# One-hot weights with tokens innermost, and expert and last-layer sums kept by tokens

## The chip, the cores and the metric

The program runs on one core of a Trainium2 chip. The metric is device time in microseconds (us). Three runs of the kernel before took 1616.15, 1618.21 and 1618.53 us; the median is 1618.21 us. The names of the engines are those of the profile: PE is TensorE (PEld its weight loads), DVE VectorE, ACT ScalarE, POOL GpSimd, SP the queue that issues the DMAs.

## The reference

Two transformer blocks run on 256 tokens with 1024 features, in float32.

The first block has a gated convolution and a chunkwise mLSTM, then the layer `peer`: 8 heads each pick 16 of 16384 experts per token. With `u` and `v` the two expert tables it computes

```
z   = einsum('thkd,td->thk', take(u, e), h)
a   = gelu(z) * g                      # g: softmax weights of the picked experts
out = einsum('thk,thkd->td', a, take(v, e))
x   = x + g2 * rms_norm(out, norm2_post)
```

The second block is stick-breaking attention beside a gated linear recurrence, then an MLP, `x = x + square(relu(rms_norm(x) @ w_up)) @ w_down`, whose result is the output.

## The kernel before

**Layout and arithmetic.** An activation is held with features on the 128 partitions and the 256 tokens along the free dimension, as 8 slices of 128x256. A float32 product is made of three matmuls in the format fp32r: a weight piece of 128x1024 is read by DMA (`raw`), ACT rounds it to a high half `wh` (line 164), and DVE, or POOL for the pieces named in `pool_`, subtracts to get the low half `wl` (line 165). `mm3` (lines 184 to 186) then adds wh·xh, wh·xl and wl·xh. Three `wh`/`wl` buffers rotate.

**The peer layer.** The kernel doesn't gather experts; it goes densely through all 16384 in 128 chunks of 128. `z_chunk` (line 847) makes the 128x256 scores of a chunk with 24 matmuls (`gemm`) and ACT applies gelu. `out_chunks` (line 1063) splits a scaled chunk into `ah`, `al` and adds its part of the output with `acc_k` (line 238): for each of 8 feature slices three matmuls, the weights being 128x128 pieces of `wh` or `wl`, the moving operand the 256 tokens of `ah` or `al`. The sums stand in four PSUM banks, two feature slices of 128x256 in each.

Between the two the scores are multiplied by the routing weights of each token and expert. `weights_of(s, n)` (line 1016) builds them for n groups of 32 chunks, in 16 blocks of TB=16 tokens: DVE makes a one-hot `o1` of the first key with the keys innermost (line 1023), a one-hot `o2` of the second key with the tokens innermost (line 1027) and `og`, two products of `o2` with the high and the low part of the weight (line 1031). For each token one fp16 matmul (line 1038) has `o1` of this token as weights and both parts of `og` as moving operand, 64 columns with n=1 and 128 with n=2; neighbouring columns of `og` are 16 elements (32 bytes) apart. ACT reads one part from PSUM (line 1041), DVE adds the other (line 1042) and multiplies into the scores (line 1046).

`weights_of` is a generator: each `advance(bg, n)` after a chunk runs it on by n steps (n may be a fraction, which is saved up), and `drain(bg)` runs what is left. It has 3 steps a block with n=1 and 4 with n=2. The order is: z chunks 44 to 95 with weights_of(0,1) and 1 step a chunk (NW), drain; out chunks 0 to 31 and z chunks 96 to 127 with weights_of(1,2) and 0.8 steps a chunk (NX), drain; out chunks 32 to 95 with weights_of(3,1) and 1 step (NY), drain; out chunks 96 to 127. These are the stretches from about 558 to 740, 740 to 994, 994 to 1163 and 1163 to 1298 us of the profile.

**The end of the peer layer.** Squares of the eight slices are summed (`presum`, `sums`), the norm is made on one row per token and spread to 128 partitions by matmuls (`norm`, with `fill` matmuls around it, F2), and `residual` adds the slices to x; `scaled` makes the halves of the next gemm's input (lines 321 and 322). The first six weight pieces of that gemm have their low halves made on POOL (LB), and their casts are ordered behind steps of the norm.

**The last layer.** The MLP makes 32 chunks of hidden features, `acc_k` adds them to the output (line 1353), and `finish` (line 1364) multiplies the sums of two slices by the norm `r4`, adds x and issues the output DMA, in the order in which the last two chunks' matmuls end. The output is written with features on partitions and turned on the host.

The instructions of each engine run in its program order; `issue_after` puts one behind another where the code says so.

Of the kernel before, what the change touches and what calls it, by code (L numbers as in the profile page):

```python
# [111 lines left out]
def body(ctx: ExitStack, tc: tile.TileContext, a: dict):  # L112
# [705 lines left out]
    with ExitStack() as p2:  # L818
# [197 lines left out]
        def weights_of(s, n):  # L1016


            m = 32 * n
            for b in range(S // TB):  # L1020
                ts_ = slice(b * TB, (b + 1) * TB)
                o1 = op_.tile([128, TB, 128], F16, tag="o1", name="o1", bufs=2)
                V.tensor_tensor(out=o1, in0=row16[:, None, :].to_broadcast([128, TB, 128]),  # L1023
                                in1=idxT[:, 0, ts_, None].to_broadcast([128, TB, 128]), op=ALU.is_equal)
                yield
# [3 lines left out]
                og = op_.tile([128, 2, 64, TB], F16, tag="og", name="og", bufs=2)[:, :, :m]  # L1029
                for i in range(2):  # L1030
                    V.tensor_tensor(out=og[:, i], in0=o2, in1=gT[:, i, None, ts_].to_broadcast([128, m, TB]),
                                    op=ALU.mult)
                yield
                nt = 8 // n
                for k in range(TB // nt):
                    ps = gt().rearrange("p (t i n) -> p t i n", i=2, n=m)
                    for t in range(nt):
                        T.matmul(ps[:, t], lhsT=o1[:, k * nt + t, :], rhs=og[:, :, :, k * nt + t], start=True, stop=True)  # L1038
                    t0 = b * TB + k * nt
                    u = m2.tile([128, 256], F32, tag="u", name="u", bufs=2).rearrange("p (n t) -> p n t", t=nt)  # L1040
                    A.activation(u, ps[:, :, 0].rearrange("p t n -> p n t"), AF.Copy, scale=1.0 / GS)
                    V.scalar_tensor_tensor(out=u, in0=ps[:, :, 1].rearrange("p t n -> p n t"), scalar=1.0 / GS, in1=u,  # L1042
                                           op0=ALU.mult, op1=ALU.add)
                    for q_ in range(n):
                        zz = zt[s + q_][:, :, t0:t0 + nt]
                        V.tensor_mul(zz, zz, u[:, 32 * q_:32 * q_ + 32])
                    if k % 2:
                        yield
# [56 lines left out]
        total = presum(m2, acc, 6)
        last, mm = sums(m2, ssy, acc, total, 6)
        add = added[0]
        ry, _, root, inv, end = norm(m2, ssy, gt(), mm, F2)
        places = dict(q=(A, last), r=(A, root), e=(A, end), a=(V, add), i=(V, inv), n=(A, None))
        hh3, hl3 = halves()  # L1110
        residual(m2, x, acc, ry, prm[:, 24:32], lambda j: scaled(x, KS("n12"), hh3, hl3, j))

    with ExitStack() as p3:
# [223 lines left out]
        for n in range(32):  # L1339
# [11 lines left out]
            if 0 < n < 30 or n == 31:  # L1351
                k = min(n - 1, 29)
                acc_k(acc, (next(cd), mid[k]), first=k == 0)
            if n == 4:
                total = presum(m3, x)
            if n == 8:
                ssx = pz.tile([128, 384], F32, tag="zr", name="ssx", bufs=1)[:, :256]
                squares(m3, ssx, x, total)
                r4 = m3.tile([128, 256], F32, name="r4")
                V.tensor_scalar(out=r4, in0=ssx, scalar1=1.0 / D, scalar2=EPS, op0=ALU.mult, op1=ALU.add)  # L1360
# [1 line left out]
        adds = []

        def finish(j):

            if j in (0, 2, 4):
                return
            at = slice(j if j > 5 else j - 1, j + 1)
            n = at.stop - at.start
            y = (zs8, e8)[j // 2 % 2].rearrange("p h c t -> p (h c t)")[:, :n * 256].rearrange("p (j t) -> p j t", j=n)  # L1370
            with tc.issue_after(adds[-1].ins) if adds else ExitStack():
                V.tensor_tensor(out=y, in0=acc.t[j // 2][:, at.start % 2:at.start % 2 + n], op=ALU.mult,
                                in1=r4[:, None, :].to_broadcast([128, n, 256]))
            adds.append(V.tensor_add(x[:, at], x[:, at], y))
            SY.dma_start(out=a["out"].rearrange("p (j t) -> p j t", j=8)[:, at], in_=x[:, at])

        acc_k(acc, *[(next(cd), mid[k]) for k in (30, 31)], last=True, order=(6, 0, 1, 2, 3, 4, 5, 7), then=finish)


# [105 lines left out]
```

## Time and profile before

| what | us |
|---|---|
| runs: lowest, median, highest | 1616.15, 1618.21, 1618.53 |
| the profiled execution's own time | 1615.83 |
| its span | 1614.0 |
| PE busy | 1536.8 |
| DVE busy | 1235.1 |
| ACT busy | 762.0 |
| POOL busy | 243.6 |

The mean granted TensorE clock of the profiled execution is 0.972 of full speed. The span goes from the first to the last instruction that the profile records; 1.8 us of the execution lie outside. Busy times are sums over an engine's instructions where they overlap only once. Matmuls are pipelined, so one is recorded with some 280 ns although the next starts after some 118 ns: the rate is read from the starts of neighbours, not from the durations.

### The profile page before, as it was taken

How to read it: one execution, taken by the hardware profiler on the slowest of the kernel's cores; microseconds unless marked ns; L12 is line 12 of the kernel's file. 1: busy time of each engine (PE TensorE's matmuls, PEld its weight loads, DVE VectorE, ACT ScalarE, POOL GpSimd, SP SyncE). 2: the span in 40 equal slices, each digit the busy share in tenths (PEclk: the TensorE clock that was granted, in tenths of full speed). 3: DMA queues.
4: the chain of work that ended last, by engine and by line, in shares of the span. 5: the costliest groups of instructions: out<-in, count | busy, mean ns of one | idle time of the engine just before them, and what ended most of it. 6: DMA issues, size and time to landing. Idle time of an engine off the chain costs nothing.

```text
span 1614.0 us, 29532 instructions
## 1 busy us (share of the span) xinstructions
PE 1536.8 (95%) x12164; PEld 1475.0 (91%) x12164; DVE 1235.1 (77%) x2231; ACT 762.0 (47%) x1263; POOL 243.6 (15%) x109
## 2 busy tenths in 40 slices
PE   5899999989888999999999997999999989999998
PEld 4898899979888999999899985999999979899998
DVE  8978796677969999887877778888755578666555
ACT  3544454445435434444444443444444458754442
POOL 3300000034436843330000000000000030000000
PEclk7999999999999999999999997999999989999999
DMA  9456594534433534444434341444455535344542
GB/s 347 178 196 240 204 336 175 185 120 169 168 132 134 182 134 153 150 144 161 173 134 154 134 156 51 157 153 145 159 191 190 183 121 183 105 155 186 183 184 79
DMA packets 40025, 269.82 MB, mean 167 GB/s; under 512 B 4433, under 2 KB 5201, under 8 KB 9170
## 3 DMA queue, kind: packets, MB, share of 16 engines
q1 hardware_dynamic: 38882, 264.67, 45.5%
q10 hardware_dynamic: 1008, 3.27, 0.6%
q8 instruction: 95, 1.56, 0.4%
q14 instruction: 40, 0.33, 0.1%
HBM read 266.87 MB, written 1.05 MB: 166 GB/s over the span
## 4 chain that ended last, share of the span: by engine, by line
PE 83%; DVE 14%; ACT 2%; issue 1%; DMA 0%; SPq 0%; DVEq 0%; ACTq 0%
PE mm L184 12%; PE mm L186 12%; PE mm L185 12%; PE acc L185 10%; PE acc L186 10%; PE acc L184 10%; PE g L1038 7%; DVE wl L165 1%; DVE cand L877 1%; DVE scr L411 1%; DVE x L342 1%; DVE pr L917 1%; DVE o L1023 1%; PE mm L218 1%; DVE i L871 1%
## 5 line engine op out<-in xcount | busy, mean ns | idle before, releaser
L164 ACT CAST wh<-raw 128x1024 fp32r<-128x1024 f32 x449 | 470.0, 1049 | 623.6 <-PE mm L185 315.1
L165 DVE TENSOR_TENSOR wl<-raw,wh 128x1024 fp32r<-128x1024 f32 x361 | 441.8, 1229 | 175.8 <-ACT wh L164 173.1
L186 PE MATMUL mm<-hh,wl 128*128 128x256 f32 x1816 | 516.4, 284 | 12.3 <-DVE wl L165 12.0
L184 PE MATMUL mm<-hh,wh 128*128 128x256 f32 x1816 | 521.5, 287 | 4.4 <-ACT z L854 4.4
L185 PE MATMUL mm<-hl,wh 128*128 128x256 f32 x1816 | 513.4, 283 | 0.0
L186 PEld LDWEIGHTS mm<-hh,wl 128*128 128x128 f32 x1816 | 346.6, 191 | 15.0 <-DVE wl L165 13.7
L184 PEld LDWEIGHTS mm<-hh,wh 128*128 128x128 f32 x1816 | 345.9, 190 | 11.3 <-ACT z L854 4.6
L185 PEld LDWEIGHTS mm<-hl,wh 128*128 128x128 f32 x1816 | 346.6, 191 | 0.8 <-issue 0.2
L165 POOL TENSOR_TENSOR wl<-raw,wh 128x1024 fp32r<-128x1024 f32 x89 | 227.1, 2558 | 492.5 <-PE mm L312 252.8
L184 PE MATMUL acc<-ah,wh 128*128 128x256 f32 x1024 | 289.4, 283 | 2.0 <-ACT ah L248 2.0
L185 PE MATMUL acc<-al,wh 128*128 128x256 f32 x1024 | 288.6, 282 | 0.0
L186 PE MATMUL acc<-ah,wl 128*128 128x256 f32 x1024 | 288.4, 282 | 0.0
L184 PEld LDWEIGHTS acc<-ah,wh 128*128 128x128 f32 x1024 | 194.6, 190 | 3.9 <-ACT ah L248 2.5
L185 PEld LDWEIGHTS acc<-al,wh 128*128 128x128 f32 x1024 | 193.9, 189 | 0.3
L186 PEld LDWEIGHTS acc<-ah,wl 128*128 128x128 f32 x1024 | 193.3, 189 | 0.0
L1023 DVE TENSOR_TENSOR o<-row,idxT 128x2048 f16<-128x2048 f16 x48 | 123.7, 2577 | 66.1 <-PE g L1038 66.1
L1038 PE MATMUL g<-og,o 128*128 128x64 f16 (+1 forms) x768 | 129.9, 334 | 12.2 <-DVE u L1042 6.5
L1038 PEld LDWEIGHTS <-o 128*128 128x128 f16 x768 | 83.0, 115 | 38.9 <-issue 8.1
L1138 POOL MEMSET q<- 128x2048 f32 x1 | 1.8, 1809 | 557.7 <-DVE al L249 557.7
L185 PE MATMUL acc<-ml,wh 128*128 128x256 f32 x256 | 72.3, 283 | 0.0
L186 PE MATMUL acc<-mh,wl 128*128 128x256 f32 x256 | 72.2, 282 | 0.0
L184 PE MATMUL acc<-mh,wh 128*128 128x256 f32 x256 | 71.9, 282 | 0.0
(435 smaller groups left out, 2194.9 us busy)
## 6 DMA issues: line engine op xcount, KB each, us to landing
raw<-in_uT_dram SPq DMA_DIRECT2D x64, 1024.0 KB, 4.8
raw<-in_ev_dram SPq DMA_DIRECT2D x64, 1024.0 KB, 4.8
araw<-in_wada_dram SPq DMA_DIRECT2D x16, 1024.0 KB, 5.8
raw<-in_wup_dram SPq DMA_DIRECT2D x16, 1024.0 KB, 4.7
raw<-in_wdn_dram SPq DMA_DIRECT2D x16, 1024.0 KB, 4.8
raw<-in_wcxb_dram SPq DMA_DIRECT2D x12, 1024.0 KB, 4.8
araw<-in_wada_dram SPq DMA_DIRECT2D x16, 512.0 KB, 9.9
raw<-in_wout_dram SPq DMA_DIRECT2D x8, 1024.0 KB, 4.8
```

The costliest lines, as they stand in the source:

```text
L164: by.copy(wh, raw) if by is A else by.tensor_copy(wh, raw)
L165: on.tensor_sub(wl, raw, wh)
L184: T.matmul(ps, lhsT=wh, rhs=xh, start=start, stop=False, skip_group_check=skip)
L185: T.matmul(ps[:, :n], lhsT=wh, rhs=xl, start=False, stop=False, skip_group_check=skip)
L186: return T.matmul(ps, lhsT=wl, rhs=xh, start=False, stop=stop, skip_group_check=skip)
L218: T.matmul(ps, lhsT=w, rhs=xh[:, k, :n], start=k == 0, stop=False)
L342: V.tensor_add(x[:, j, :], x[:, j, :], u)
L411: return V.scalar_tensor_tensor(out=scr, in0=raw, scalar=0.5, in1=crow, op0=ALU.mult, op1=ALU.mult, accum_out=ada[:, j:j + 1])
L871: V.max_index(out=ti[:, i, 8:16], in_max=tv[:, i, 8:16], in_values=rep)
L877: V.tensor_add(cand[:, :, o:o + n], tv2[:, :, 0, ra:ra + 1].to_broadcast([128, 2, n]), tv2[:, :, 1, 0:n])
L1023: V.tensor_tensor(out=o1, in0=row16[:, None, :].to_broadcast([128, TB, 128]), in1=idxT[:, 0, ts_, None].to_broadcast([128, TB, 128]), op=A ...
L1038: T.matmul(ps[:, t], lhsT=o1[:, k * nt + t, :], rhs=og[:, :, :, k * nt + t], start=True, stop=True)
```

## The change

The one-hot of the first key is made by DVE with the tokens innermost (`os`) and turned by an ACT copy into `o1`; the weighted one-hots are made by one DVE instruction for both parts (`ow`) and turned by ACT into `og`, whose columns then lie side by side. The block is 8 tokens. Per token there are two matmuls, one for each part, which add up in PSUM, so that one DVE instruction scales the sum and multiplies it into the scores; ACT's read of PSUM is gone. A block is made one block ahead of its matmuls, and a generator has 64 steps. POOL no longer makes low halves after piece 49 of `uT`.

The sums of the experts and of the last layer are kept by tokens: `acc_tok` has a 128x128 piece of `xh` or `xl` (128 tokens) as weights and 512 columns of `wh` or `wl` as moving operand, 12 matmuls a chunk. The end of the peer layer takes the norm per token half with ACT's accumulated squares, scales, turns the result back with 16 transposes, and adds it to x in halves of 128 tokens. The last layer turns x instead (`turn`, 16 transposes and 8 ACT copies during chunks 12 to 19), and writes its output by tokens.

```diff
-TB = 16
+TB = 8
-LB = ('qaee',(0,1,2,3,4,5))
+LB = ('', ())
-F2 = (5,10)
+F2 = 10
-NZ, NR, NW, ZR, NX, NY = (7, 1.75, 1, 44, 0.8, 1)
+NZ, NR, NW, ZR, NX, NY = (7, 1.75, 1.25, 44, 1.05, 1.05)
+    def acc_tok(acc, *steps, first=False, last=False, then=lambda t, c: None):
+        for t in range(2):
+            ts_ = slice(t * 128, (t + 1) * 128)
+            for c in range(2):
+                cs = slice(c * 512, (c + 1) * 512)
+                for n, ((wh, wl), (xh, xl)) in enumerate(steps):
+                    T.matmul(acc[t][c], lhsT=xh[:, ts_], rhs=wh[:, cs], start=first and n == 0, stop=False)
+                    T.matmul(acc[t][c], lhsT=xl[:, ts_], rhs=wh[:, cs], start=False, stop=False)
+                    T.matmul(acc[t][c], lhsT=xh[:, ts_], rhs=wl[:, cs], start=False, stop=last and n == len(steps) - 1)
+                then(t, c)
...
         def weights_of(s, n):
             m = 32 * n
-            for b in range(S // TB):
-                o1 = op_.tile([128, TB, 128], F16, tag="o1", name="o1", bufs=2)
-                V.tensor_tensor(out=o1, in0=row16[:, None, :].to_broadcast([128, TB, 128]),
-                                in1=idxT[:, 0, ts_, None].to_broadcast([128, TB, 128]), op=ALU.is_equal)
...
+            def made_of(b):
+                os = op_.tile([128, 128, TB], F16, tag="os", name="os", bufs=1)
+                V.tensor_tensor(out=os, in0=io16, in1=idxT[:, 0, None, ts_].to_broadcast([128, 128, TB]),
+                                op=ALU.is_equal)
+                o1 = op_.tile([128, TB, 128], F16, tag="o1", name="o1", bufs=2)
+                A.copy(o1, os.rearrange("p n t -> p t n"))
                 o2 = ...
+                ow = op_.tile([128, 2, 64, TB], F16, tag="ow", name="ow", bufs=1)[:, :, :m]
+                V.tensor_tensor(out=ow, in0=o2[:, None].to_broadcast([128, 2, m, TB]),
+                                in1=gT[:, :, None, ts_].to_broadcast([128, 2, m, TB]), op=ALU.mult)
+                og = op_.tile([128, TB, 128], F16, tag="og", name="og", bufs=2)[:, :, :2 * m]
+                og = og.rearrange("p t (i n) -> p t i n", i=2)
+                A.copy(og, ow.rearrange("p i n t -> p t i n"))
+                return o1, og
+            blocks = S // TB
+            next_ = made_of(0)
+            yield
+            for b in range(blocks):
+                o1, og = next_
+                if b + 1 < blocks:
+                    next_ = made_of(b + 1)
+                    yield
+                ps = gt()[:, :TB * m].rearrange("p (t n) -> p t n", t=TB)
+                for t in range(TB):
+                    for i in range(2):
+                        T.matmul(ps[:, t], lhsT=o1[:, t, :], rhs=og[:, t, i], start=i == 0, stop=i == 1)
+                for q_ in range(n):
+                    zz = zt[s + q_][:, :, b * TB:(b + 1) * TB]
+                    V.scalar_tensor_tensor(out=zz, in0=ps[:, :, 32 * q_:32 * q_ + 32].rearrange("p t n -> p n t"),
+                                           scalar=1.0 / GS, in1=zz, op0=ALU.mult, op1=ALU.mult)
                 yield
-        cu = chunks(a["uT"], range(64), pool_={*range(50), *range(50, 96, 2)})
+        cu = chunks(a["uT"], range(64), pool_={*range(50)})
...
-                acc_k(acc, *steps, first=i == 0, last=i == 127)
+                acc_tok(acc, *steps, first=i == 0, last=i == 127, then=ended if i == 127 else lambda t, c: None)
...
+        def ended(t, c):
+            A.activation(yt[:, t, c * 512:(c + 1) * 512], acc[t][c], AF.Square, accum_out=rt[:, t, c:c + 1])
+            if c == 0:
+                return
+            V.tensor_add(rt[:, t, 2:3], rt[:, t, 0:1], rt[:, t, 1:2])
+            A.activation(rt[:, t, 3:4], rt[:, t, 2:3], AF.Sqrt, bias=epsc, scale=1.0 / D)
+            V.reciprocal(rt[:, t, 4:5], rt[:, t, 3:4])
+            A.activation(yt[:, t, 0:512], acc[t][0], AF.Copy, scale=rt[:, t, 4:5])
+            V.tensor_scalar(out=yt[:, t, 512:1024], in0=acc[t][1], scalar1=rt[:, t, 4:5], scalar2=None, op0=ALU.mult)
...
+        for t in range(2):
+            for j in range(8):
+                T.transpose(turned[t][j // 4][:, j % 4 * 128:j % 4 * 128 + 128], yt[:, t, j * 128:(j + 1) * 128], C("ident"))
+            if t == 0:
+                fill(mmt(), F2)
+            for j in range(8):
+                V.scalar_tensor_tensor(out=x[:, j, ts_], in0=turned[t][j // 4][:, j % 4 * 128:j % 4 * 128 + 128],
+                                       scalar=prm[:, 24 + j:25 + j], in1=x[:, j, ts_], op0=ALU.mult, op1=ALU.add)
+                if t == 1:
+                    scaled(x, KS("n12"), hh3, hl3, j)
...
-                acc_k(acc, (next(cd), mid[k]), first=k == 0)
+                acc_tok(acc, (next(cd), mid[k]), first=k == 0)
+            if 12 <= n < 20:
+                turn(n - 12)
+        def finish(t, c):
+            for h in range(2):
+                at = slice(c * 512 + h * 256, c * 512 + h * 256 + 256)
+                V.scalar_tensor_tensor(out=xt[:, t, at], in0=acc[t][c][:, h * 256:h * 256 + 256], scalar=r4[:, t:t + 1],
+                                       in1=xt[:, t, at], op0=ALU.mult, op1=ALU.add)
+                if h or (t, c) == (1, 1):
+                    SY.dma_start(...)
```

## Rows read from the trace of the kernel before

**Rows 1.** The page: PE's busy line, and the chain's shares by line.

```profile
PE 1536.8 (95%) x12164; PEld 1475.0 (91%) x12164; DVE 1235.1 (77%) x2231; ACT 762.0 (47%) x1263; POOL 243.6 (15%) x109
...
PE mm L184 12%; PE mm L186 12%; PE mm L185 12%; PE acc L185 10%; PE acc L186 10%; PE acc L184 10%; PE g L1038 7%; DVE wl L165 1%; DVE cand L877 1%; DVE scr L411 1%; DVE x L342 1%; DVE pr L917 1%; DVE o L1023 1%; PE mm L218 1%; DVE i L871 1%
```

**Rows 2.** Windows: length; busy PE, PEld, DVE, ACT, POOL; granted clock; DMA; GB/s.

```profile
558.00:740.00 182.00, 178.80 (x1490) 177.87 (x1489) 164.94 (x170) 79.89 (x139) 72.17 (x27) 0.98 0.42 148
740.00:970.00 230.00, 230.00 (x1751) 208.26 (x1750) 172.84 (x293) 102.71 (x175) 0.00 (x0) 1.00 0.43 152
970.00:994.40 24.40, 13.43 (x55) 6.26 (x53) 21.16 (x53) 7.72 (x19) 0.00 (x0) 0.60 0.05 19
...
1298.00:1327.00 29.00, 21.31 (x144) 20.08 (x144) 22.73 (x36) 14.48 (x31) 14.68 (x6) 0.76 0.38 132
```

**Rows 3.** Single lines: duration in ns, lowest/median/highest; first and last start.

```profile
L1038 PEld LDWEIGHTS <-o x768: 95/117/128, 569.2 to 1162.0; 128*128 128x128 f16 x192
L1038 PE MATMUL g<-og,o x768: 275/298/413, 569.2 to 1162.1; 128*128 128x64 f16 x128, 128*128 128x128 f16 x64
...
L1301 PEld LDWEIGHTS o<-zs,v x16: 133/134/137, 1390.2 to 1412.0; 128*64 128x64 f32 x16
...
L1011 PEld LDWEIGHTS g<-sk,qT x64: 186/192/192, 373.8 to 483.4; 128*128 128x128 f32 x64
...
L1161 PE MATMUL rows<-sq,ca x16: 377/379/381, 1326.9 to 1345.0; 128*104 128x256 f32 x16
```

**Rows 4.** Timeline of PE: start, length (us), line; first and last of 94 between 1200 and 1212.

```profile
623.34 2.04 PE L1038 MATMUL g<-og,o 128*128 128x64 f16 x16
...
757.10 2.02 PE L1038 MATMUL g<-og,o 128*128 128x128 f16 x8
...
1200.08 0.28 PE L184 MATMUL acc<-ah,wh 128*128 128x256 f32 x1
...
1211.03 0.28 PE L184 MATMUL acc<-ah,wh 128*128 128x256 f32 x1
...
1298.61 0.97 PEld L294 LDWEIGHTS mm<-ones,sq 128*128 128x128 f32 x8
...
1327.75 1.46 PE L1161 MATMUL rows<-sq,ca 128*104 128x256 f32 x6
```

**Rows 5.** DVE by line and shape, 740 to 970 us: busy us, mean ns, idle before.

```profile
L165 DVE TENSOR_TENSOR wl<-raw,wh 128x1024 fp32r<-128x1024 f32 x65 | 78.7, 1220 | 25.5 <-ACT wh L164 25.5
L1023 DVE TENSOR_TENSOR o<-row,idxT 128x2048 f16<-128x2048 f16 x12 | 27.5, 2292 | 28.4 <-PE g L1038 28.4
...
L1042 DVE SCALAR_TENSOR_TENSOR u<-g,u 128x256 f32<-128x256 f32 x50 | 19.2, 416 | 1.5 <-ACT u L1041 1.5
L1031 DVE TENSOR_TENSOR og<-o,gT 128x1024 f16<-128x1024 f16 x25 | 16.1, 683 | 0.0
```

**Rows 6.** The same, 558 to 740 us, where POOL works too.

```profile
L1023 DVE TENSOR_TENSOR o<-row,idxT 128x2048 f16<-128x2048 f16 x18 | 54.9, 3053 | 16.0 <-PE g L1038 16.0
```

**Rows 7.** ACT's groups over the span, and one DVE line with a strided read.

```profile
L164 ACT CAST wh<-raw 128x1024 fp32r<-128x1024 f32 x449 | 470.0, 1049 | 623.6 <-PE mm L185 315.1 <-PE acc L185 181.7 <-issue 110.2
...
L248 ACT CAST ah<-z 128x256 fp32r<-128x256 f32 x128 | 50.6, 399 | 2.3 <-DVE z L1046 2.3
...
L1014 ACT COPY scs<-g 128x512 f32<-128x512 f32 x8 | 4.3, 596 | 1.7 <-PE g L1011 1.7
...
L1089 DVE COPY row<-io x1: 282/282/282, 561.3 to 561.3; 128x128 f16<-128x128 f16 x1
```

**Rows 8.** Timeline behind the peer layer, 1298 to 1327 us.

```profile
1299.88 14.68 POOL L165 TENSOR_TENSOR wl<-raw,wh 128x1024 fp32r<-128x1024 f32 x6 [8.64 <-ACT wh L164]
...
1302.57 4.76 DVE L342 TENSOR_TENSOR x<-x,u 128x256 f32<-128x256 f32 x2
```

**Rows 9.** Timeline of the last microseconds.

```profile
1609.35 0.28 PE L186 MATMUL acc<-mh,wl 128*128 128x256 f32 x1
...
1610.75 0.42 DVE L1374 TENSOR_TENSOR x<-x,e 128x256 f32<-128x256 f32 x1
```

More of the change, by code (lines that the diff above doesn't have):

```diff
@@ L33 @@
 LA = ('nnre',(2,3))
-LB = ('qaee',(0,1,2,3,4,5))
+LB = ('', ())
 KO = 3
-F2 = (5,10)
+F2 = 10
 KA = 0
 KB = 2
-PU = (4,50,1)
-NZ, NR, NW, ZR, NX, NY = (7, 1.75, 1, 44, 0.8, 1)
+NZ, NR, NW, ZR, NX, NY = (7, 1.75, 1.25, 44, 1.05, 1.05)
 RUNS = [(a, 16 // (a + 1)) for a in range(8)]
@@ L1028, in weights_of @@
                                 in1=idxT[:, 1, None, ts_].to_broadcast([128, m, TB]), op=ALU.is_equal)
[L1029 to L1032, printed above, removed]
-                yield
[L1034 to L1048, printed above, removed]
@@ L1087, in body @@
         zq.append(op_)
-        row16 = op_.tile([128, 128], F16, name="row16")
-        V.tensor_copy(row16, io16[:, :, 0])
         bg = [weights_of(0, 1)]
@@ L1092, in body @@
         drain(bg)
-        acc = Banks(pacc)
+        acc = [[pacc.tile([128, 512], F32, tag=f"acc{2 * t + c}", name="acc") for c in range(2)] for t in range(2)]
+        rt = m2.tile([128, 2, 5], F32, name="rt")
+        def ended(t, c):
[7 more added lines that the diff above has]
+            V.tensor_scalar(out=yt[:, t, 512:1024], in0=acc[t][1], scalar1=rt[:, t, 4:5], scalar2=None, op0=ALU.mult)
         bg = [weights_of(1, 2)]
@@ L1100, in body @@
         drain(bg)
+        yt = zq[1].tile([128, 32, 256], F32, tag="z1", name="yt")[:, :8].rearrange("p (t j) n -> p t (j n)", t=2)
         out_chunks(96, 128)
-        ssy = mmt(258)
         raws = [load(a["wqk2"][b]) for b in range(2)]
[L1105 to L1109, printed above, removed]
-        hh3, hl3 = halves()
-        residual(m2, x, acc, ry, prm[:, 24:32], lambda j: scaled(x, KS("n12"), hh3, hl3, j))
+        hh3, hl3 = halves()
+        turned = [[gt() for _ in range(2)],
+                  [pacc.tile([128, 512], F32, tag=f"acc{i}", name="turned") for i in range(2)]]
+        for t in range(2):
+            ts_ = slice(t * 128, (t + 1) * 128)
+            for j in range(8):
+                T.transpose(turned[t][j // 4][:, j % 4 * 128:j % 4 * 128 + 128], yt[:, t, j * 128:(j + 1) * 128],
+                            C("ident"))
+            if t == 0:
[5 more added lines that the diff above has]
+                    scaled(x, KS("n12"), hh3, hl3, j)
     with ExitStack() as p3:
@@ L1146, in body @@
         rows = psl.tile([104, 256], F32, name="rows")
-        cqk = chunks(a["wqk2"], range(4), raws, {i: places[t] for i, t in enumerate(LB[0])}, LB[1])
+        cqk = chunks(a["wqk2"], range(4), raws, {}, LB[1])
         pss, ws = [mmt(), mmt(), pz.tile([128, 384], F32, tag="o", name="mm3", bufs=1)[:, :256],
@@ L1329, in body, with turn @@
             scaled(x, KS("n22"), hh, hl, j)
-        acc = Banks(pacc)
+        acc = [[pacc.tile([128, 512], F32, tag=f"acc{2 * t + c}", name="acc") for c in range(2)] for t in range(2)]
+        xt = zs8.rearrange("p h c t -> p (h c t)")[:, :2048].rearrange("p (t n) -> p t n", t=2)
+        def turn(i):
+            t, q = divmod(i, 4)
+            pt = pz.tile([128, 384], F32, tag=("o", "zr")[i % 2], name="pt", bufs=1)
+            for k in range(2):
+                T.transpose(pt[:, k * 128:(k + 1) * 128], x[:, 2 * q + k, t * 128:(t + 1) * 128], C("ident"))
+            A.copy(xt[:, t, q * 256:(q + 1) * 256], pt[:, :256])
         cu, cd = chunks(a["wup"], range(16)), chunks(a["wdn"], range(16))
@@ L1356, in body @@
             if n == 8:
[L1357 to L1360, printed above, removed]
+                ssx = pz.tile([128, 384], F32, tag="zr", name="ssx", bufs=1)
+                sums(m3, ssx, x, total, 8)
+                r4 = m3.tile([128, 2], F32, name="r4")
+                V.tensor_scalar(out=r4, in0=ssx[:, 256:258], scalar1=1.0 / D, scalar2=EPS, op0=ALU.mult, op1=ALU.add)
                 V.reciprocal(r4, r4)
[L1362 to L1377, printed above, removed]
+            if 12 <= n < 20:
[6 more added lines that the diff above has]
+                if h or (t, c) == (1, 1):
+                    at = slice(at.start if (t, c) == (1, 1) else c * 512, at.stop)
+                    SY.dma_start(out=a["out"].rearrange("p (t n) -> p t n", t=2)[:, t, at], in_=xt[:, t, at])
+        acc_tok(acc, *[(next(cd), mid[k]) for k in (30, 31)], last=True, then=finish)
 def layout(x, c, w_ada, b_ada, norm1_pre, norm1_post, w_in, conv_a_w, conv_qk_w, b_igate, b_fgate, mh_norm_w,
@@ L1482 @@
     r = _run(nc, [arrays], core_ids=[0])
-    o = r.results[0]["out_0_dram"].reshape(128, 8, 256)
-    return np.ascontiguousarray(o.transpose(2, 1, 0)).reshape(1, 256, 1024)
+    o = r.results[0]["out_0_dram"].reshape(128, 2, 1024)
+    return np.ascontiguousarray(o.transpose(1, 0, 2)).reshape(1, 256, 1024)
```

1 line of the change is left out of this document (removed).

## The prediction

> **What bounds the kernel now.** I read the page's busy lines and the chain's shares first: PE is busy 95% of the span, and the chain lies on it almost throughout, 7% of it (113 us) in the one-hot matmuls of line 1038 and 30% in the matmuls that sum into `acc` [rows 1]. The windows come second, since a mean over stages hides two holes. In 558 to 970 us PE has no idle time but the first 3.2 us; in 970 to 994.4, the drain of weights_of(1,2), it is busy 13.4 of 24.4 us and the granted clock is 0.60; in 1298 to 1327, behind the peer layer, it is busy 21.3 of 29.0 at 0.76 [rows 2]. DVE is at 91% in the first stage, where POOL works beside it, and at 75% in the second; ACT is at 44 to 45% [rows 2]. So a saving counts where it shortens PE's own work or closes a hole, and ACT has room. The rates of PE come last, from the starts of neighbours in the timeline: 117.7 ns for an fp32r matmul of 256 columns (10.95 us over 93 intervals), 116 ns for a one-hot matmul of 64 columns ((2.04 - 0.298)/15) and 230 ns for one of 128 ((2.02 - 0.413)/7) [rows 3, 4]. A column of the strided one-hots thus costs 1.78 ns, one of the packed fp32r operand 0.46.
>
> **1. One-hot matmuls.** Before: 512 at 0.116 and 256 at 0.230 us are 118.3 us, on the path. After: 3 x 256 tokens x 2 parts = 1536 matmuls of 32 or 64 packed columns. At 0.46 ns the columns take 15 to 29 ns, so the weight load decides. A load of 64 fp32 columns is recorded with 134 ns, of 128 with 192, so 0.9 ns a column and 76 fixed; the fp16 load of 128 columns has 95 to 117 and so occupies 19 to 41 ns [rows 3]. Lower bound 35 ns a pair; upper bound 111 ns, the spacing of fp32 loads whose matmul has one column ((0.97 - 0.19)/7) [rows 4]. I take 50, near the fp16 load itself with some handing over: 76.8 us. Change -41.5 (-64.5 to +52).
>
> The Trainium skill (TensorE: Matmul & The Clock Gate, back-to-back issue gap) gives about 81 ns for a sustained pair of weight load and matmul of 128 columns; by that, an estimate, the sum here would be 124 us and the change +6. No row of this case has packed fp16 columns to test it.
>
> **2. The drain.** weights_of(1,2) has 16 x 4 = 64 steps and got 0.8 x 64 = 51; the other 13 run uncovered, 24.4 us, of which 54 one-hot matmuls at 0.230, 12.4 us, are counted in step 1. Now 64 steps meet 1.05 x 64 = 67 advances. Change -12.0 (the rest of the window [rows 2]). The first stage's block is made two chunks before its matmuls, so the idle 3.2 us there go: -3. But with 1.25 x 52 = 65 advances the last block of that stage now ends with its last chunk, and out chunk 0 waits for the multiply into the scores (0.42) and for `ah` (0.40) and `al` (0.42) [rows 5, 7]: some 1.5 to 2.5 us, I take +2.
>
> **3. DVE and ACT in these stages.** Per block of 8 tokens DVE now has `os` (1024 elements, as line 1031's 0.68), `o2` and `ow` (together 768 or 1536 elements: 0.7 or 1.1) and one or two multiplies from PSUM (0.42 each) [rows 5]: 1.8 us with n=1, 2.6 with n=2. Stage one: 32 x 1.8 = 58 and 46 low halves x 1.22 = 56, 114 of some 173 us, against 165 of 182; without POOL the stretching goes too (line 1023 took 3.05 there and 2.29 without POOL) [rows 5, 6]. Nothing of DVE comes onto the path, nor do POOL's 23 pieces that DVE takes over.
> ACT gains two copies a block. A contiguous cast costs 0.18 + 0.846 ns an element (1049 for 1024, 399 for 256) [rows 7]; `o1` 1.05, `og` 1.05 (n=2) or 0.61 (n=1). But these copies read 16 bytes apart. The nearest row with such a read is DVE's line 1089, 128 elements 32 bytes apart in 282 ns; line 1042 takes 416 for 256, so 128 more cost 1.05 ns each and no penalty shows in the strided read [rows 5, 7]. I take 1.05. Stage two then: 64 x 1.45 + 32 x 2.1 = 160 of 205 us. Cost 0 under PE. If the cover went: at PE's 1.78 ns a column the copies take 2.0, 2.0 and 1.1 us; stage two has 93 + 128 = 221 us of ACT against 205 of PE, stage one 174 against 173, stage three 192 against 203, so +15 to +20.
>
> On this the Trainium skill (SBUF — State Buffer, cachelines, under Door 1) says that SBUF has lines of 16 bytes and that an access which crosses to a new line each time pays. PE's strided columns bear it out (1.78 against 0.46 ns), DVE's strided copy does not; for ACT no row shows it.
>
> **4. Sums by tokens.** 24 matmuls of 256 columns become 12 of 512. Lower bound: an fp32 matmul of 256 columns streams for 216 ns ((1.46 - 0.38)/5), 0.84 ns a column, and shows no further cost [rows 3, 4]; if 512 fp32r columns took the same, 19.4 ns a pair would go, -37 over 12 x 160. Upper bound 0: 235.4 = 2 x 117.7. Why is 117.7 more than half of 216? The strided one-hots suggest a reading rate: 64 columns, each in a stretch of its own, take 116 ns, and 64 x 16 bytes of fp32r take 117.7. If 16 bytes per 1.78 ns is the limit, 512 columns take 230 as the 128 strided ones did. I take 231: -4.5 ns x 12 x 128 = -6.9 for the experts, -1.7 for the last layer's 32 chunks.
>
> **5. Behind the peer layer.** From the last sum (T) 29 us pass, with 96 gemm matmuls (11.4 us) in them [rows 2]. DVE stands behind POOL there: six low halves on POOL over 14.7 us, two adds of line 342 in 4.76 us instead of 0.8 [rows 8]. After: square 0.6, three small steps 0.6, scaling 0.6 (as line 1014) [rows 7], transposes 8 x 0.11, with hand-overs some 3.4 us; the first token half has all this behind the second half's matmuls. Then 8 times an add (0.28) and a low half (0.42 to 0.48) on DVE: T + 9.5; four low halves of the weights (4.9) in between or before: up to T + 14.4; the gemm's low pass is 32 x 0.118 = 3.8 more: T + 13.3 to 18.2, and 2 for a low clock. I take T + 20: -9 (-14 to 0). No part of POOL's stall is late next; DVE is.
>
> **6. Last layer.** `turn` puts 16 transposes at 0.11 on PE: +1.8; its ACT copies lie under PE (ACT is busy 47% of the span [rows 1]). At the end the last matmul starts at 1609.35 and the last add ends at 1611.17 [rows 9]; now two fused adds of 0.42 follow the last matmul: -0.6. Five output DMAs as before.
>
> **Sum.** -41.5 - 12 - 3 + 2 - 6.9 - 1.7 - 9 + 1.8 - 0.6 = -70.9; I keep 3 of it back for edges, as there are 96 bursts of one-hots instead of 64 and each costs PE a hand-over. -68 from the profiled execution's own 1615.83 gives 1548; the median of the runs lies 2.4 above that, so 1550.
>
> **Rivals.**
> - *512 columns stream at the fp32 rate.* 216 to 224 ns instead of 231: -13 to -29 more, about 1525. For it: the fp32 row has no extra cost beyond its columns. Against: the strided and the packed rows fit one reading rate. The Trainium skill's gap for an isolated stream (TensorE page, same section), N/2.4 + 2.5, would give 216.
> - *ACT's turned reads cost a line each.* Step 3: 1550 + 18 = 1568. The Trainium skill's rule on cachelines (step 3) would bring this; for it speaks PE's strided row, against it DVE's.
> - *The wait only moves: ACT's queue.* The copy of `os` waits for DVE, up to 1.9 us behind a weight piece, and the weight casts, the head of PE's supply, queue behind it. Three buffers cover two chunks, 5.65 us, less 2.27 for cast and low half and 0.4 for `ah`: 3.0. A wait of 1.9 and copies of 2.1 (1.67 with n=1) exceed it by 1.0 (0.6): at worst 32 x 1.0 + 64 x 0.6 = 70 us, all of the gain; half of that is 1585. Against it: ACT's idle time and one block of lead.
> - *The matmuls double and each load costs in full.* Every token's `o1` is loaded twice. At 111 ns a pair the one-hots take 170 us, 94 more than in the forecast: 1644, slower. It decides from a break-even of 50 + 68/1.536 = 94 ns a pair. Against it: the fp16 load is recorded with 95 to 117 ns where fp32 has 192.
>
> **How the numbers follow.** Forecast 0.43, first rival 0.20, ACT's reads 0.16, ACT's queue 0.13, full loads 0.08. The forecast's own range is 1530 to 1572, from 40 to 60 ns a pair and 5 us either way behind the peer layer. The range 1512 to 1595 takes in the first three rivals but for the worst half of ACT's queue. Within 0.2% (about what runs of this kernel can tell from no change) needs ACT's queue near its worst or a pair near 94 ns: 0.03; slower is the last rival and little else: 0.08; faster 0.89.
>
> **What would show it.** One-hot bursts: 16 matmuls in 0.8 us, first start to last, is right; over 1.3 makes the forecast wrong. acc matmuls: 231 ns from start to start; 216 is the first rival. ACT's copy of 1024 fp16: 1.05, or 2.0 for the second rival. No window like 970 to 994.4. PE idle between 558 and 1298 over 10 us means ACT's queue. From the last expert matmul to the end of the next gemms: 20 us.

## Result and the profile after

The changed kernel takes 1533.28 us (median of 4 runs, 1532.91 to 1534.84) against 1618.35 (1616.15 to 1618.53) before: ratio 0.9479, 95% interval 0.9463 to 0.9496. The forecast was 1550 with a range of 1512 to 1595. The side is right and the range holds the time, but the 17 us between the forecast and the time are more than these runs scatter, and the terms show that two large ones were wrong in opposite directions. The profiled execution took 1533.28 us itself, 82.55 less than the 1615.83 of the one before; the terms below are set against that.

The page of the changed kernel: busy time of the engines, and ACT in 40 slices of the span (tenths). PE answers to [rows 1].

```profile
PE 1463.7 (96%) x11020; PEld 1329.1 (87%) x11020; DVE 1132.0 (74%) x2160; ACT 1021.7 (67%) x1338; POOL 166.2 (11%) x80
...
ACT  3554354445443559999999999999964569554542
```

PE's share has hardly moved, yet ACT has gone from 47% to 67%, and in the 16th to the 29th slice (574 to 1110 us, the stages with one-hots) it is busy 90% or more. The windows (columns as in [rows 2]) say it in us:

```profile
558.00:1225.00 667.00, 656.75 (x5118) 572.72 (x5117) 484.71 (x763) 592.40 (x629) 14.78 (x7) 0.99 0.50 170
...
740.00:940.00 200.00, 194.40 (x1620) 170.54 (x1619) 155.87 (x252) 198.94 (x187) 0.00 (x0) 1.00 0.48 164
...
1225.54:1245.26 19.72, 17.95 (x135) 17.23 (x134) 16.64 (x41) 15.23 (x33) 0.00 (x0) 0.91 0.45 160
```

In 740 to 940 ACT is busy 198.9 of 200 us, and PE, which had no idle time there before [rows 2], has 5.6. From 558 us to the end of the expert sums PE's idle time is 10.2 us, just over the 10 that the prediction gave as the sign of ACT's queue. The third line is the stretch from the last expert matmul to the end of the next gemms, 19.7 us long. What fills ACT are its groups over the span (as [rows 7]):

```profile
L163 ACT CAST wh<-raw 128x1024 fp32r<-128x1024 f32 x450 | 473.1, 1054 | 378.0 <-PE mm L184 190.5 <-PE acc L254 96.6 <-issue 48.4
L1040 ACT COPY o<-os 128x1024 f16<-128x1024 f16 x96 | 198.0, 2063 | 0.0
L1049 ACT COPY og<-ow 128x512 f16<-128x512 f16 x64 | 72.5, 1133 | 0.8 <-DVE ow L1045 0.8
L1049 ACT COPY og<-ow 128x1024 f16<-128x1024 f16 x32 | 65.7, 2052 | 0.0
```

A turned copy of 1024 elements takes 2.06 us, not 1.05; one of 512 takes 1.13, not 0.61. Together they are 336 us. Next the one-hot line by itself, loads and matmuls (answering [rows 3]):

```profile
L1063 PEld LDWEIGHTS <-o x1536: 95/96/104, 568.8 to 1128.1; 128*128 128x128 f16 x192
L1063 PE MATMUL g<-og,o x1536: 176/176/203, 570.7 to 1128.1; 128*128 128x32 f16 x128, 128*128 128x64 f16 x64
```

The rates come from PE's timeline (start, length), as in [rows 4]:

```profile
570.68 0.59 PE L1063 MATMUL g<-og,o 128*128 128x32 f16 x16 [2.90 <-ACT og L1049]
...
614.03 0.28 PE L185 MATMUL mm<-hh,wl 128*128 128x256 f32 x1
614.15 0.56 PE L1063 MATMUL g<-og,o 128*128 128x32 f16 x16
614.56 0.39 PE L183 MATMUL mm<-hh,wh 128*128 128x256 f32 x1
...
732.68 0.49 PE L253 MATMUL acc<-wh,ah 128*128 128x512 f32 x1 [0.90 <-ACT ah L260]
734.02 0.50 PE L254 MATMUL acc<-wh,al 128*128 128x512 f32 x1 [0.85 <-DVE al L261]
...
782.77 0.40 PE L255 MATMUL acc<-wl,ah 128*128 128x512 f32 x1
783.01 0.64 PE L1063 MATMUL g<-og,o 128*128 128x64 f16 x16
783.49 0.48 PE L253 MATMUL acc<-wh,ah 128*128 128x512 f32 x1
...
1179.80 0.39 PE L253 MATMUL acc<-wh,ah 128*128 128x512 f32 x1
...
1199.99 0.40 PE L253 MATMUL acc<-wh,ah 128*128 128x512 f32 x1
...
1225.54 0.39 PE L255 MATMUL acc<-wl,ah 128*128 128x512 f32 x1
...
1241.29 3.97 PE L222 MATMUL mm<-hh,wl 128*128 128x256 f32 x32
...
1527.23 0.39 PE L255 MATMUL acc<-wl,mh 128*128 128x512 f32 x1
```

Inside a burst a pair of load and matmul takes (0.56 - 0.176)/15 = 25.6 ns with 32 columns and (0.64 - 0.194)/15 = 29.7 with 64 (0.194 is that form's mean). From the first start to the last a burst takes 0.38 or 0.45 us, where the prediction gave 0.8 as the sign of being right. With its edges a burst costs more: from the end of the matmul before it (614.31) to the end of the one behind (614.95) are 0.64 us, of which 0.118 belong to that one, so 0.52 a burst; with 64 columns 0.80 - 0.232 = 0.57. The 88 matmuls of 512 columns from 1179.80 to 1199.99 stand 20.19/87 = 232 ns apart. PE still waits 2.90 us before the first burst and 0.90 + 0.85 where the sums begin. Three stretches can be told apart by ACT's gelu of chunk 43, the last before the one-hots, and the last expert matmul. The lines are from the kernel before and from the changed kernel:

```profile
557.43 0.38 ACT L854 ACTIVATE z<-mm 128x256 f32<-128x256 f32 x1
1297.83 0.28 PE L186 MATMUL acc<-ah,wl 128*128 128x256 f32 x1
```

```profile
562.09 0.38 ACT L866 ACTIVATE z<-mm 128x256 f32<-128x256 f32 x1
```

From the gelu to the last expert matmul (1225.54 in the changed kernel) 740.4 us have become 663.4. At the end (as [rows 9]) the last add follows the last matmul:

```profile
1527.66 0.48 DVE L1418 SCALAR_TENSOR_TENSOR zs<-acc,r,zs 128x256 f32<-128x256 f32 x1 [0.52 <-PE acc L255]
```

### The profile page after: what moved, and what is told of

It reads as the page before. It is cut to its first block, busy times and chain, and to the rows that moved or that the text cites. A ratio compares the mean times of both kernels' runs of the same rounds, so it can differ in the third digit from the quotient of the medians.

```text
span 1531.5 us, 27307 instructions
## 1 busy us (share of the span) xinstructions
PE 1463.7 (96%) x11020; PEld 1329.1 (87%) x11020; DVE 1132.0 (74%) x2160; ACT 1021.7 (67%) x1338; POOL 166.2 (11%) x80
## 3 DMA queue, kind: packets, MB, share of 16 engines
HBM read 266.61 MB, written 1.05 MB: 175 GB/s over the span
## 5 line engine op out<-in xcount | busy, mean ns | idle before, releaser
L253 PE MATMUL acc<-wh,ah 128*128 128x512 f32 x512 | 205.9, 402 | 1.9 <-ACT wh L163 1.0
L255 PE MATMUL acc<-wl,ah 128*128 128x512 f32 x512 | 202.5, 395 | 0.7 <-DVE wl L164 0.5
L254 PE MATMUL acc<-wh,al 128*128 128x512 f32 x512 | 202.0, 395 | 0.8 <-DVE al L261 0.8
L1040 ACT COPY o<-os 128x1024 f16<-128x1024 f16 x96 | 198.0, 2063 | 0.0
L164 POOL TENSOR_TENSOR wl<-raw,wh 128x1024 fp32r<-128x1024 f32 x60 | 149.6, 2501 | 396.4 <-PE mm L324 252.9
L1049 ACT COPY og<-ow 128x512 f16<-128x512 f16 (+1 forms) x96 | 138.2, 1439 | 0.8 <-DVE ow L1045 0.8
L255 PEld LDWEIGHTS acc<-wl,ah 128*128 128x128 f32 x512 | 96.2, 188 | 26.8 <-DVE wl L164 4.7
L253 PEld LDWEIGHTS acc<-wh,ah 128*128 128x128 f32 x512 | 96.2, 188 | 22.6 <-ACT wh L163 1.4
L254 PEld LDWEIGHTS acc<-wh,al 128*128 128x128 f32 x512 | 96.1, 188 | 21.6 <-DVE al L261 1.2
L1037 DVE TENSOR_TENSOR os<-io,idxT 128x1024 f16<-128x1024 f16 x96 | 66.7, 694 | 54.6 <-ACT o L1040 54.6
```

The lines of the kernel that those rows point to most:

```text
L164: on.tensor_sub(wl, raw, wh)
L253: T.matmul(acc[t][c], lhsT=xh[:, ts_], rhs=wh[:, cs], start=first and n == 0, stop=False)
L254: T.matmul(acc[t][c], lhsT=xl[:, ts_], rhs=wh[:, cs], start=False, stop=False)
L255: T.matmul(acc[t][c], lhsT=xh[:, ts_], rhs=wl[:, cs], start=False, stop=last and n == len(steps) - 1)
L1037: V.tensor_tensor(out=os, in0=io16, in1=idxT[:, 0, None, ts_].to_broadcast([128, 128, TB]), op=ALU.is_equal)
L1040: A.copy(o1, os.rearrange("p n t -> p t n"))
```

## Experiments

All times are medians of 4 runs; the kernel before had medians of 1617.9 to 1618.9 in the three groups of runs, so they stand side by side. The stretch up to the gelu of chunk 43 is 3.4 to 5.8 us longer in the profiles of these versions than in the kernel before, though no edit below changes it; so 1 or 2 us between two versions say little by themselves. Theory A after the result: the one-hots are some 27 us cheaper than forecast, and ACT's turned reads give about 15 of it back. The rivals stand with each run.

**ACT's reads in line.** Both copies read in storage order, so this version leaves the turning out:

```
-  A.copy(o1, os.rearrange("p n t -> p t n"))
+  A.copy(o1, os.rearrange("p n t -> p (n t)").rearrange("p (t n) -> p t n", t=TB))
   (og likewise, in two halves of its columns)
```

> ACT's two copies a block read their source in line instead of 16 bytes apart; the turning is left out, so the one-hots are not the right ones, everything else runs as in the changed kernel. Theory A (the turned reads make ACT the bound: it is busy 199 of 200 us in 740 to 940): the copies of 1024 elements fall from 2.06 to 1.05 us, the one of 512 from 1.13 to 0.6, ACT's busy time between 740 and 940 falls to about 135, PE's 6 us of idle time there and the delays of its matmuls around the bursts go, 1533 becomes 1521 to 1525. Theory B (PE is the bound all the same, ACT's queue only looks full): copies shorter, but 1533 within 2. Theory C (the first block of each stage costs it, not the load): only the idle time at 568 to 571 shrinks by 1.5 us, 1531.

1516.69 us (ratio to before 0.9375, 0.9359 to 0.9391), 16.6 below the changed kernel. Its windows, the two marks of the stretch with one-hots, and ACT's groups from 560 to 1200 us:

```profile
558.00:1210.00 652.00, 649.61 (x5111) 570.14 (x5111) 486.19 (x762) 444.81 (x630) 13.79 (x6) 1.00 0.51 173
...
740.00:940.00 200.00, 200.00 (x1688) 178.77 (x1687) 162.46 (x260) 147.95 (x195) 0.00 (x0) 1.00 0.51 170
```

```profile
560.92 0.38 ACT L866 ACTIVATE z<-mm 128x256 f32<-128x256 f32 x1
1209.96 0.39 PE L255 MATMUL acc<-wl,ah 128*128 128x512 f32 x1
```

```profile
L1040 ACT COPY o<-os 128x1024 f16<-128x1024 f16 x96 | 99.8, 1039 | 1.3 <-DVE os L1037 1.3
...
L1049 ACT COPY og<-ow 128x512 f16<-128x512 f16 x64 | 39.5, 617 | 1.8 <-DVE ow L1045 1.8
L1049 ACT COPY og<-ow 128x1024 f16<-128x1024 f16 x32 | 33.4, 1044 | 0.0
```

With the copies at the forecast's durations ACT is at 148 of 200 us (A had 135) and PE has no hole in that window; the waits at 732 are gone too, and PE's idle time falls from 10.2 to 2.4 us. The time lies 4 us below A's band, far from B's and C's. The stretch with one-hots takes 649.0 us instead of 663.4, so in the profiles the turned reads cost 14.4 us; the other 2 of the 16.6 are the stretch ahead (1.2) and the scatter of the runs.

**Every pair twice.**

```
-  for t in range(TB):
+  for t in [t for t in range(TB) for _ in range(2)]:
```

> Every burst of one-hot matmuls is issued twice into the same place (the second starts the sums anew), so 1536 more pairs of load and matmul. From the spacing within a burst, (0.56 - 0.177)/15 = 25.5 ns with 32 columns and (0.64 - 0.194)/15 = 29.7 with 64, theory A expects 1024 x 25.5 + 512 x 29.7 = 41 us more on PE, less what the ACT-bound stretches swallow (up to 8): 1566 to 1574. Theory B (a pair really costs 50 ns as forecast, the starts in the trace hide it): plus 77, 1610. Theory C (ACT is the bound in all three stages, PE has free time for it): less than 10 more.

1562.32 us, 29.0 more: below A's band, far from B and C. A predicted that ACT's bound would swallow up to 8; by A's own 41 it was 12. The clean price needed a version in which ACT is no bound; it follows below.

**DVE writes turned.** In one kernel the gate product, in the other the first one-hot goes straight to its place, without ACT:

```
-  V.tensor_tensor(out=ow, in0=...)  ;  A.copy(og, ow.rearrange("p i n t -> p t i n"))
+  V.tensor_tensor(out=og.rearrange("p t i n -> p i n t"), in0=...)

-  V.tensor_tensor(out=os, in0=io16, ...)  ;  A.copy(o1, os.rearrange("p n t -> p t n"))
+  V.tensor_tensor(out=o1.rearrange("p t n -> p n t"), in0=io16, ...)
```

> The product of one-hot and gate is written by DVE straight into the turned place (its writes 256 bytes apart, its reads in line), and ACT's second copy is gone. ACT loses 138 us over the three stages. Theory A (ACT's load is the bound): ACT's busy time between 740 and 940 falls to about 135; if DVE's scattered write costs no more than its reading (0.69 us for 1024), 1521 to 1525; if it goes to 1.1 us or so, DVE rises to 170 of 195 us and it is still 1522 to 1527. Theory B (PE is the bound): 1533 within 2. Theory C (a scattered write costs DVE a line an element, 2 us for 1024): DVE is full in the second stage and the time is 1533 to 1545.

> The first one-hot is written by DVE straight into the turned place and ACT's first copy is gone (198 us of ACT over the three stages). Theory A: ACT falls to about 135 of 200 us in the second stage and to about 80 of 142 in the first; 1520 to 1525 if DVE's 1024 elements take up to 1.2 us instead of 0.69. Theory B: 1533 within 2. Theory C (2 us on DVE): DVE full in the second stage, 1533 to 1545.

1637.3 and 1768.33 us, 1.2% and 9.4% above the kernel before (ratios 1.012, 1.010 to 1.0141, and 1.0935, 1.0917 to 1.0953). No theory had this size; C had the direction. The second stage and DVE's groups from 560 to 1400 us, first with the product, then with the first one-hot written turned:

```profile
740.00:940.00 200.00, 154.62 (x971) 122.96 (x970) 195.56 (x182) 102.71 (x109) 0.00 (x0) 0.89 0.33 111
```

```profile
L1046 DVE TENSOR_TENSOR og<-o,gT 128x512 f16<-128x512 f16 x64 | 163.4, 2553 | 0.1
L1046 DVE TENSOR_TENSOR og<-o,gT 128x1024 f16<-128x1024 f16 x32 | 153.9, 4810 | 0.0
```

```profile
740.00:940.00 200.00, 155.56 (x1063) 127.50 (x1062) 195.18 (x173) 96.86 (x112) 0.00 (x0) 0.87 0.33 110
```

```profile
L1037 DVE TENSOR_TENSOR o<-io,idxT 128x1024 f16<-128x1024 f16 x96 | 462.5, 4818 | 0.0
```

4.8 us instead of 0.69 for 1024 elements written 256 bytes apart, 4.7 ns an element. The two say nothing on ACT's load, since DVE became the bound (196 and 195 of 200 us); they show what turning by DVE's writes would have cost. PE, left waiting, was granted 0.89 and 0.87 of its clock there instead of 1.00, so a part of these times is the clock's.

**Turned in fours and in twos.** The tokens of a block lie in groups of TT = 4 or 2, so that ACT reads 8 or 4 bytes apart:

```
+  q = TB // TT
-  os = op_.tile([128, 128, TB], ...)      ;  A.copy(o1, os.rearrange("p n t -> p t n"))
+  os = op_.tile([128, q, 128, TT], ...)   ;  A.copy(o1 as (q t) n, os.rearrange("p q n t -> p q t n"))
   (o2, ow and og likewise; ow in two DVE instructions)
```

> The one-hots lie with four tokens innermost (8 bytes) and two such groups outside, so ACT reads 8 bytes apart instead of 16; the gate product becomes two DVE instructions. Theory A (ACT pays for each 16 bytes it comes to anew, two reads share one): the copy of 1024 elements takes about (1.04 + 2.06)/2 = 1.55 us, ACT's busy time in the second stage falls from 199 to some 170 of 195 us, and of the 16.6 us between the changed kernel and the one with reads in line 10 to 16 come back: 1517 to 1524. Theory B (any step other than one costs the same): 2.06 us still, 1533 to 1536. DVE's 1024 elements stay at 0.69 us in both if its reading in fours costs nothing; if it falls to one element at a time (1.1 us or more), 5 us worse.

> The same with two tokens innermost (4 bytes), four groups outside: ACT reads 4 bytes apart. Theory A: four reads share 16 bytes, a copy takes 1.04 + 1.02/4 = 1.3 us, ACT is no bound any more, 1516 to 1520 if DVE keeps its 0.69 us. Theory B: 2.06 us, 1533 to 1536. What may spoil it: DVE's operands have two elements in a row only; at 1.1 us for 1024 it is at 180 of 195 us in the second stage, 1518 to 1524.

1518.72 us (ratio 0.9385, 0.937 to 0.9401) and 1519.16 (0.9388, 0.9372 to 0.9404). ACT from 560 to 1140 us, first in fours, then in twos, and the second stage in fours:

```profile
L1042 ACT COPY o<-os 128x1024 f16<-128x1024 f16 x96 | 108.3, 1129 | 1.5 <-DVE os L1039 1.5
```

```profile
L1042 ACT COPY o<-os 128x1024 f16<-128x1024 f16 x96 | 99.8, 1040 | 1.7 <-DVE os L1039 1.7
```

```profile
740.00:940.00 200.00, 200.00 (x1681) 178.97 (x1678) 163.69 (x294) 154.15 (x197) 0.00 (x0) 1.00 0.50 170
```

The times fall in A's bands and B's 2.06 us is out, but A's formula fails: 1129 and 1040 ns, where it had 1550 and 1300. The two costs don't add; the longer counts. With 0.18 us fixed [rows 7], 16 bytes apart are 1.83 ns an element and in line 0.84. If each new 16 bytes cost 1.83 ns, two elements share it in fours: 0.915 x 1.024 + 0.18 = 1.12 us, and 1.13 were measured; in twos it is 0.46, below ACT's own 0.84.
The Trainium skill (SBUF — State Buffer, cachelines, under Door 1) asks for two or more hits in each line of 16 bytes for full bandwidth; these three durations agree but for 8%: one hit 2063 ns, two 1129, four 1040.

**DVE copies, reading turned.** `V.tensor_copy` instead of `A.copy` for `og`.

> The second turned copy is DVE's instead of ACT's, still reading 16 bytes apart and writing in line. DVE's line with a read 32 bytes apart shows 282 ns for 128 elements, 1.05 ns an element: 1.2 us for 1024, 0.65 for 512. Theory A (ACT is the bound, and DVE pays for scattered writes, not for scattered reads): DVE rises in the second stage by 32 x 1.2 = 38 us to 194 of 200 and is nearly full, ACT falls to 135; 1520 to 1530. Theory B (DVE pays for scattered reads as for scattered writes, 4.8 us): as slow as the version that writes turned, about 1637.

1522.2 us (0.9407, 0.9391 to 0.9422). DVE from 560 to 1140 us, and the second stage:

```profile
L1049 DVE COPY og<-ow 128x512 f16<-128x512 f16 x64 | 39.9, 623 | 0.1
L1049 DVE COPY og<-ow 128x1024 f16<-128x1024 f16 x32 | 34.8, 1087 | 0.0
```

```profile
740.00:940.00 200.00, 200.00 (x1687) 178.82 (x1686) 187.62 (x291) 151.80 (x163) 0.00 (x0) 1.00 0.51 172
```

A holds, though ACT is at 152 of 200 us and not at 135: it still takes 2.06 us for its remaining copy, but PE has no idle time in this window, so it was the load that cost. DVE's copies, 1087 and 623 ns for 1024 and 512 elements 16 bytes apart, were expected at 1.2 and 0.65 us; their difference is 0.91 ns an element, half of ACT's 1.83.

**The experts' sums and their end as before.** `acc_tok` back to `acc_k`, with the old code behind the peer layer.

> The experts' sums and what follows the peer layer as in the kernel before (256 columns, transposed sums, the stretch with POOL); new one-hots and new last layer stay. Theory A (from the starts in the trace: 231.7 ns for 512 columns against twice 117.7, so 1536 x 3.7 = 6 us; and 19.7 us behind the peer layer against 29.2): 1533 + 15 = 1546 to 1551. Theory B (the one-hots are worth what was forecast, and the surplus comes from 512 columns): 1533 + 37 or more, 1570.

1548.37 us (0.9568, 0.9552 to 0.9584), 15.1 above the changed kernel; A. PE's timeline behind the peer layer:

```profile
1232.30 0.28 PE L185 MATMUL acc<-ah,wl 128*128 128x256 f32 x1
...
1257.67 3.96 PE L222 MATMUL mm<-hh,wl 128*128 128x256 f32 x32
```

That stretch is 29.3 us again, 9.6 over the changed kernel's 19.7; 5.5 are left for the sums, where the spacing gives 1536 x (235.4 - 232.1) = 5.1. B, which gave the surplus to 512 columns, is out.

**The last layer as before.** `acc_k` and the old `finish`; no `turn`.

> The changed kernel with the last layer of before (256 columns, sums transposed, end in pieces of one or two of the eight). Theory A (the working of step 6, with what the trace shows): 384 matmuls of 512 columns are worth 384 x 3.7 ns = 1.4 us, the 16 transposes cost 1.8 and the end gains 0.6, so nothing: 1532 to 1535. Theory B (the end with two fused adds is worth more than the trace shows): 1536 to 1540.

1533.37 us, 0.1 from the changed kernel: A's band. In its profile the time behind the first gemms after the peer layer is 0.9 us longer (287.2 us instead of 286.2), and the stretch ahead is 0.7 us shorter, so the last layer's change is worth some 0.9 us at most.

**One matmul a token where n = 1**, on top of fours; **every pair twice in fours**; and the first with a later start:

```
+  if n == 1:   T.matmul(ps[:, t], lhsT=o1[:, t, :], rhs=og[:, t], start=True, stop=True)   (64 columns)
+               u = ACT copy of the first half; V: u += second half; V: z *= u

   (pairs twice: the line of the second experiment)

+  if s == 0:  yield      (after made_of(0); NW 1.25 -> 1.3)
```

> On top of the version turned in fours (1518.7): in the two stages with n=1 a token has one matmul of 64 columns instead of two of 32 that are summed in PSUM; the two halves are added as before by ACT and DVE (a copy of 0.4 us and one more DVE instruction of 0.42 a block). Theory A (a pair costs the longer of the load, 25.5 ns, and the columns, 29.7 for 64): 1024 x 25.5 = 26.1 us become 512 x 29.7 = 15.2, minus 11: 1506 to 1510. Theory B (a burst costs PE its hand-over, not its pairs): minus 3 at most, 1515 to 1519. Theory C (the longer chain PE, ACT, DVE, DVE holds the PSUM buffer and PE waits): 1519 or slower.

> The version turned in fours with every burst of one-hots issued twice, so that ACT is no bound under it. Theory A: the whole price of the pairs shows now, 1024 x 25.5 + 512 x 29.7 = 41 us: 1557 to 1561; the 29 us over the changed kernel were less because ACT's bound swallowed 12. Theory B (the pairs themselves cost 29/1536 = 19 ns): 1548 again.

> As the version with one matmul a token in fours, and the matmuls of the first block of all wait one chunk longer, so that ACT's two copies are done before PE comes to them. PE's 2.8 us of idle time before the first one-hots go, the stage has one step more (1.3 instead of 1.25 a chunk): 2 to 3 us below the version without it, 1504 to 1507, if theory A of that one holds. If the wait only moves (to the end of the stage, where the last block's product comes with the last chunk), the same time as without.

One matmul a token: 1509.23 us (0.9324, 0.9309 to 0.934), 9.5 below fours; A's 11, less 1.5. Pairs twice in fours: 1559.13, 40.4 more against 41: A, 26.3 ns a pair over 1536, so the spacing in the trace is the price, and the missing 12 of the second experiment lay in ACT's bound. Late start: 1505.44 us (0.93, 0.9284 to 0.9315), 3.8 below the one without, where 2 to 3 were expected; the fastest version here, 27.8 below the changed kernel. PE's first bursts of that version:

```profile
571.21 0.39 PE L1070 MATMUL g<-og,o 128*128 128x64 f16 x8
572.43 0.39 PE L184 MATMUL mm<-hh,wh 128*128 128x256 f32 x1 [0.83 <-ACT z L867]
```

No idle time stands before the first burst now; 0.83 us follow it, so 2.0 of the 2.83 us without the late start are gone. The clock bears on the rest. From 570 to 577 us, first without and then with the late start (columns as in [rows 2]):

```profile
570.00:577.00 7.00, 6.08 (x35) 6.08 (x35) 5.61 (x13) 5.09 (x8) 2.38 (x1) 0.51 0.47 150
```

```profile
570.00:577.00 7.00, 6.14 (x56) 5.91 (x56) 5.62 (x9) 5.97 (x9) 4.42 (x2) 1.00 0.44 150
```

After 2.83 us of idle time the granted clock is 0.51, the lower of its two levels (1.2 GHz), and some 24 matmuls of 256 columns stand 0.213 us apart instead of 0.118: 2.3 us, which the expectation didn't count. With the late start it is 1.00. Together that is 4.3 us, of which 3.8 show in the runs.

## Why the prediction was right, and where it was wrong

| term | forecast | measured | from |
|---|---|---|---|
| 1. one-hot matmuls | -41.5, edges +3 | -70 | medians with edges: 32 bursts of 1.89 and 32 of 1.86, 120 us, before; 64 of 0.50 and 32 of 0.56, 50 us, after |
| 2. drain; start; stage end | -12, -3, +2 | -14, 0, in 3 | no such window, nor the low clock behind it; 2.90 us still idle |
| 3. ACT's copies | 0 | +14.4 | reads in line, chunk 43 to the last expert matmul |
| 4. experts' sums | -6.9 | -5 | 232 ns; sums as before |
| 5. behind the peer layer | -9 | -9.5 | 29.2 us [rows 2, 8] to 19.7 |
| 6. last layer | -0.5 | -0.8 | 287.0 us to 286.2; last layer as before |
| ahead of the change | 0 | +4.7 | gelu of chunk 43: 557.43, now 562.09 |
| sum | -68 | -80; the whole is -82.5 | |

Some 2 us of the gain are in no term and weren't followed further. That the part ahead of the change is longer is seen in every profile of a version with it (3.4 to 5.8 us at chunk 43); its cause wasn't sought and stays open.

*Step 1* was mis-sized: "I take 50, near the fp16 load itself with some handing over". A pair takes 25.6 to 29.7 ns, with the burst's edges 50/1536 = 33, under the lower bound of 35. That bound is about what the load (19 to 41 ns) and the columns (15 to 29) give when their lowest values are added, but they don't add. With 32 columns the pair stands on 25.6, within the load's 19 to 41, though 32 columns at 0.46 ns are 15; with 64 it stands on 29.7, which is 64 x 0.46 and leaves nothing for a load in series. So the longer of the two counts: the load's share is at most 25.6 ns, and by these two points, an estimate, the columns decide from about 56 on. One matmul a token is the test that used this, and it gained.
The 81 ns a pair that the Trainium skill (TensorE: Matmul & The Clock Gate, back-to-back issue gap) gives for 128 columns can't be carried to 32 or 64: the measured pairs are a third of it.

*Step 3* failed: "no penalty shows in the strided read. I take 1.05". The row was DVE's, and it says nothing of ACT: DVE reads 16 bytes apart at 0.91 ns an element, ACT at 1.83, next to PE's 1.78 a column [rows 4]. The text had the other end, 2.0, 2.0 and 1.1 us, with a price of 15 to 20, and the trace shows 2.06, 2.05 and 1.13 with 14.4 to 16.6. It was held to be the less likely because one row of another engine was weighed above PE's strided columns, which pointed the other way. The chance of 0.16 was too low.

*Steps 2, 4, 5, 6* held, but for the start: the -3 there did not come. DVE's, ACT's and again DVE's pieces follow one another until 570.6, and PE still waits 2.9 us. In the changed kernel ACT's two copies are 2.05 and 1.11 us of it, not 1.05 and 0.61, and ACT waits 0.81 us between them for DVE, whose second one-hot takes 2.48 us beside a low half on POOL (0.29 at the next block):

```profile
566.45 2.42 POOL L164 TENSOR_TENSOR wl<-raw,wh 128x1024 fp32r<-128x1024 f32 x1 [1.79 <-ACT wh L163]
```

```profile
566.54 2.48 DVE L1042 TENSOR_TENSOR o<-io,idxT 128x256 f16<-128x256 f16 x1
```

```profile
569.51 1.11 ACT L1049 COPY og<-ow 128x512 f16<-128x512 f16 x1 [0.81 <-DVE ow L1045]
```

With the reads in line 2.4 us of the wait remain, so the chain itself is longer than the lead. The drain was worth 2 us more than its window, as the low clock outlasted it in the kernel before: 19 matmuls of 256 columns took 4.20 us there, where at 0.118 each they would take 2.2:

```profile
994.40:998.60 4.20, 4.20 (x19) 4.20 (x20) 4.20 (x8) 0.86 (x3) 0.00 (x0) 0.50 0.00 0
```

Of the rivals, 512 columns at 216 to 224 ns and full loads are refuted by the spacing. The wait that moves into ACT's queue came true in a small part: PE's idle time between 558 us and the last sum is 10.2 us and falls to 2.4 with reads in line, so it is part of the 14.4 and not a price of its own. So 1533 lies below the forecast because the larger error, some 32 us in the one-hots and their edges, was in the change's favour and the others, 14.4 us of ACT's reads and 4.7 ahead of the change, against it. That the time still fell inside the forecast's own range of 1530 to 1572 is in part luck.

## What to carry to other kernels

Where data must be turned, let the reader step at most 8 bytes, so that two fp16 share 16 bytes (ACT 1.13 instead of 2.06 us for 1024), and don't let DVE scatter its writes (4.8 us). A duration read off one engine's row prices that engine alone: before a copy goes to another engine, sum that engine's work against the window with the dearest price, here 199 of 200 us. A forecast that comes out right is checked term by term, or two errors that cancel are taken for knowledge.

## What the runs showed of the hardware that was not expected

DVE pays 4.7 ns for each fp16 element that it writes 256 bytes apart (4810 ns for 1024), while a read 16 bytes apart costs it 0.91 (1087 ns for 1024, 623 for 512). ACT's price for 16 new bytes (1.83 ns) and for an element (0.84) don't add: the longer counts. A pair of an fp16 load of 128 columns and a matmul of 32 packed columns repeats every 25.6 ns, although the load alone is recorded with 96. A hole of 2.83 us in PE's work cost 2.3 us more than its length: the granted clock was 0.51 from 570 to 577 us, and matmuls of 256 columns stood 0.213 us apart instead of 0.118.
